# Gate steps at two places of a slot, stores and copies in other slots, residual loads by GpSimd, first and last parts reordered, in a one-core decoder layer

## The chip, the cores and the metric

The kernel runs on one core of a Trainium2 chip. A core has five engines that work side by side and signal one another with semaphores: TensorE (PE in the profile; its weight loads are PEld), VectorE (DVE), ScalarE (ACT), GpSimd (POOL) and SyncE (SP). SP issues DMAs only; ACT and POOL issue some too (a line with ACTq or SPq is such an issue). Each engine takes its instructions in the order in which they stand in its queue. The metric is the device time of one execution in microseconds.

## The reference

One layer of a decoder, in f32, for 512 prompt tokens and 8 sampled tokens, 520 columns in all, with a model width of 2048 and an FFN width of 5632:

```python
def conv_ffn(xn, prev, w_up, conv_w, conv_b, w_down):
    u, v = jnp.split(xn @ w_up, 2, axis=-1)
    cu, new = causal_dwconv(u, prev, conv_w)
    h = jax.nn.silu(cu + conv_b) * v
    return h @ w_down, new

m, c_new, s_new = mixer(rmsnorm(x, norm_mix_g[l]), conv_prev[l], gla_prev[l], w_in[l], ...)
x = x + m
f, f_new = conv_ffn(rmsnorm(x, norm_ffn_g[l]), ffn_prev[l], w_up[l], ...)
x = x + f
return rmsnorm(x, final_norm_g), ...
```

`mixer` projects with `w_in`, runs a gated convolution and a gated linear attention (GLA) with a state, and projects with `w_out`. `causal_dwconv` has width 3; the last two rows of its input are outputs as well.

## The kernel before

**Products.** Every f32 operand is split in two parts, `hi` (rounded, by ACT) and `lo` (the rest, by DVE), and a product is three matmuls: hi·hi, lo·hi, hi·lo. A matmul has a stationary 128x128 block of weights and 260 moving columns, half of the 520.

**Stages.** To 68 us: x is transposed tile by tile (`x_tile`), while the first products over `w_in` (one column block of q and one of k) run over the 16 tiles, with the norm's factors and the gate's low-rank product behind. To 600 us: the rest of `w_in`, GLA and convolution. To 870: `w_out`, and sums of x for the FFN. From 871 to 1812 the FFN's up phase, to 2227 its down phase, and to 2302 the last part: the last four FFN tiles, the residual and the final norm, in two halves of the columns (`half`).

**The up phase** has 44 tiles `t`. Each is a Strassen-Winograd product: seven products of half size instead of eight, in the order 1, 5, 6, 2, 7, 3, 4 (`ORDER`). Product `i` fills a slot of 24 matmuls on PE; `r` is its number in the scheme and `j` its place, `i % 7`. The weights of some products are sums of blocks, made on DVE, one of them in place in a single buffer `s` (5 to 6 to 3). The loop writes each slot in this order:

```python
        if i:
            (up_finish if i <= NU else down_finish)(i - 1)
        (up_product if kind == "up" else down_product)(i)
        prepare(i + 2)
```

then the gate's steps that are due, then `tick()`, which flushes collected state rows. `prepare(i + 2)` splits the weights of the product two slots later: hi by ACT (L1048), the next sum (L1012) and lo (L1052) by DVE. `up_finish(i - 1)` combines the last product's bank; after r = 3 it multiplies by the norm factor R (L1132) and calls `keep_last`, whose ACT copy (L522) takes the last rows of z.

`gate(t)` is a generator with the steps of a tile after its products; its yields are numbers of slots since the slot j = 0 of the next tile. Convolution taps (ACT L459, DVE L464 and L467), Silu (L1161), v·R (L1163), h = Silu·v (L1167); on odd t four half operations that make Strassen sums of h from two tiles (L1179 to L1181, with L1057), then four calls of `stored`: hi by ACT into one of two `fh` buffers, lo by DVE, two DMAs by POOL (L1146) to `f_d`.

**The down phase** has 5 chunks c of 4 groups g of 7 products, with the operands read back from `f_d` (`load_form`, L1213) into eight slots. `load_residual` (L1227) reads the residual into accumulators, `drain` writes the remaining flat rows of the convolution state (L537), and `load_last` brings the last tiles' h back (L1239, POOL).

**Order.** The FFN loop calls `InOrder`, which holds the program's order on PE, DVE and ACT. POOL and SP are ordered by a scheduler, as is everything outside the loop. Buffers: three each for hi, lo and raw weights, eight in `tmp`, two in `fh`, one for the last part's `y`.

Of the kernel before, what the change touches and what calls it, by code (L numbers as in the profile page):

```python
# [17 lines left out]
P = 128  # L18
D = 2048
# [18 lines left out]
def trunk_kernel(  # L38
# [18 lines left out]
    class InOrder:  # L57
# [5 lines left out]
        def __init__(self):  # L63
            self.count, self.last = len(self.all()), {}
# [128 lines left out]
    xa = []  # L193
    for k in range(KD):
        if k < KD // 2:
            xa.append([(quarter(bigA, f"x{s}{k}"), quarter(b12p, f"x{s}{k}b")) for s in "hl"])
        else:
            xa.append(
                [halves(bigA.tile([P, T], F32R, tag=f"x{s}{k}", name=f"x{s}{k}")) for s in "hl"]
            )  # L200
# [38 lines left out]
    def make_masks(mkp):  # L239
        nc.vector.tensor_copy(idn8, idn)  # L240
        for s in LEVELS:
# [15 lines left out]
            nc.vector.tensor_copy(masks[s], mf)  # L257


    with ExitStack() as es:  # L260
# [41 lines left out]
        cols = (3584, 3072)  # L302
        nc.scalar.dma_start(prow[0:16, :], norm_mix_g[0].rearrange("(k p) -> k p", p=P))
        load_x(xc[0][0], 0)
        nc.scalar.dma_start(xs, x_sample)
        load_x(xc[0][1], P)
        ws = [[load(w_in, 0, 4, c0, P) for c0 in cols]]
        for j in (2, 3):
            load_x(xc[0][j], j * P)
        r0 = 16  # L310
# [9 lines left out]
        for _ in range(8):  # L320
            nc.tensor.matmul(first[0][0][:, :P], ones, ones, start=True, stop=True)

        part = sp.tile([P, 4, 7], F32, name="part")
# [8 lines left out]
        def x_tile(k):  # L332
# [55 lines left out]
        for k in range(2):  # L388
            x_tile(k)
        ws = [[parts(*r) for r in ws[0]]]  # L390
        for k in range(KD):
            c, t = k // 4, k % 4
            if t == 0 and c < 3:
                load_x(xc[c + 1], (c + 1) * 512)
                ws.append([piece(w_in, 4 * c + 4, 4, c0, P) for c0 in cols])
            for ps, w in zip(first, ws[c]):
                span(ps, w, xa, k, 4 * c, 1, KD)
            if k + 2 < KD:
                x_tile(k + 2)
            junk = tmp()  # L400
# [9 lines left out]
            if c == 1:  # L410
# [8 lines left out]
            if k == 14:  # L419
                param_columns()  # L420
        nc.vector.reduce_sum(var[:, 0:4], part, axis=mybir.AxisListType.X)
        nc.vector.reduce_sum(var[:NS, 4:5], parts_s, axis=mybir.AxisListType.X)
        rs, tn, vv = (sp.tile([P, 5], F32, name=f"rs{i}") for i in range(3))
        rsqrt(var, D, vv, rs, tn, nc.vector)
        state_columns()
# [17 lines left out]
        make_masks(sp)  # L443

# [71 lines left out]
    def keep_last(z, j, n, new_p, new_s, get=None):  # L516
# [8 lines left out]
        if jj == n - 1:  # L525
            lt, c0 = last[0], (j - n + 1) * P

            def out():
# [6 lines left out]
                for r in range(10):  # L535
                    dst = new_p[0, 0, r] if r < 2 else new_s[0, r - 2, 1]
                    nc.sync.dma_start(  # L537
# [554 lines left out]
    def up_finish(i):  # L1092
# [37 lines left out]
        elif r == 3:  # L1130
            add(z2, bk["f"], st["c"])
            nc.vector.tensor_tensor(z2, z2, R[:, HT:], op=ALU.mult)  # L1132
            keep_last(st["z"], t, 11, new_ffn_p, new_ffn_s, mm_bank)
# [3 lines left out]
    def stored(src, dst):  # L1137

        n = src.shape[1]
        hi = wxp.tile([P, T], F32R, tag="fh", name="fh")[:, :n]  # L1140
        split(src, hi, src.bitcast(F32R))
        for d, x in zip(dst, (hi.bitcast(F32), src)):
# [5 lines left out]
    def gate(t):  # L1148

        st = state.pop((t,))  # L1150
        z, v = st["z"], st["v"]
        if not t:

            nc.vector.tensor_tensor(z[:, 2 : 2 + T], z[:, 2 : 2 + T], R, op=ALU.mult)
            keep_last(z, t, 11, new_ffn_p, new_ffn_s, mm_bank)
# [7 lines left out]
        nc.vector.tensor_tensor(v[:, :T], v[:, :T], R, op=ALU.mult)  # L1163
        yield 3
# [3 lines left out]
        yield 4  # L1168
        if t >= NF - CH:
            stored(h, hl_d[t - NF + CH])  # L1170
            return
# [4 lines left out]
        i = t // 2 % 4  # L1176
        t21, t34 = tmp()[:, :T], tmp()[:, :T]
# [308 lines left out]
```

## Time and profile before

| what | us |
|---|---|
| median of three runs | 2307.78 (2306.12 to 2309.48) |
| the profiled execution's own time | 2303.64 |
| its span, from first to last instruction | 2301.9 |
| up phase, from the first to the last product with R | 912.2 to 1810.5 |

The profile was taken of a single execution, and all durations are its own. A row of a timeline has the start, the duration in us (of one piece, with its count behind), engine, line and operation, and in brackets how long the engine had been idle before it and what released it. A row of waits has the total, the number and the longest. A row of windows has the stretch, its length, then the busy us with counts of PE, PEld, DVE, ACT and POOL, the clock granted to PE, the busy share of the DMA engines and GB/s. The chain is the work that ended last, traced back.

### The profile page before, as it was taken

The numbers are of one execution on the slowest core, as the hardware profiler recorded it, in microseconds if no ns is written. First come the engines' busy times: TensorE is split into PE (matmuls) and PEld (weight loads), VectorE is DVE, ScalarE is ACT, GpSimd is POOL, SyncE is SP. The second block draws the span as 40 slices with busy tenths as digits, with TensorE's granted clock in tenths as the row PEclk, the third lists the DMA queues.
The fourth block names the chain that finished last, engine by engine and source line by source line (L and its number), as shares of the span: only waits on it lengthen the run. The fifth ranks groups of instructions, "written<-read, shape, count | busy, mean of one in ns | idle before, by whom it ended". The sixth has DMA issues, their size and how long they took to land.

```text
span 2301.9 us, 43686 instructions
## 1 busy us (share of the span) xinstructions
PE 2225.7 (97%) x18131; PEld 2189.2 (95%) x18131; DVE 1625.2 (71%) x2168; ACT 998.2 (43%) x1429; POOL 305.1 (13%) x398
## 2 busy tenths in 40 slices
PE   8999999999999999999999999999999899999996
PEld 7999999999999999999999999999998899999996
DVE  6446455543434448888888898888888778888886
ACT  5334433312223335455455455455445444444445
POOL 2113223100001212011111011111111200000110
PEclk9999999999999999999999999999999999999998
DMA  7443344333455563555555555465464876764734
GB/s 215 116 129 109 103 118 120 95 92 92 112 152 157 166 192 100 143 138 140 148 149 138 137 156 140 129 165 140 124 164 134 286 239 198 231 199 144 220 111 139
DMA packets 455683, 344.06 MB, mean 149 GB/s; under 512 B 17673, under 2 KB 429733, under 8 KB 455341
## 3 DMA queue, kind: packets, MB, share of 16 engines
q1 hardware_dynamic: 438625, 288.25, 44.4%
q0 software_dynamic: 15536, 50.80, 7.1%
q8 instruction: 142, 2.33, 0.4%
q10 hardware_dynamic: 1324, 2.23, 0.3%
q14 instruction: 56, 0.46, 0.1%
HBM read 278.15 MB, written 63.27 MB: 148 GB/s over the span
## 4 chain that ended last, share of the span: by engine, by line
PE 55%; DVE 30%; issue 6%; ACT 5%; DMA 2%; POOL 1%; SPq 0%; ACTq 0%; DVEq 0%; POOLq 0%
PE mm L133 32%; DVE lo L1052 13%; PE y L1259 6%; PE x L1259 6%; DVE s L1012 6%; ACT hi L1048 4%; PE f L1259 2%; PE e L1259 2%; DVE raw L1012 2%; PE mm L1080 2%; DVE t L464 1%; DVE t L1167 1%; PE ms L720 1%; DVE t L117 1%; DVE zpad L1132 1%
## 5 line engine op out<-in xcount | busy, mean ns | idle before, releaser
L1080 PE MATMUL mm<-yh,hi 128*128 128x260 f32 x1408 | 402.4, 286 | 4.3 <-DVE t L1060 4.3
L1080 PE MATMUL mm<-yl,hi 128*128 128x260 f32 x1408 | 399.3, 284 | 0.0
L1080 PE MATMUL mm<-yh,lo 128*128 128x260 f32 x1408 | 398.4, 283 | 0.0
L1052 DVE TENSOR_TENSOR lo<-s,hi 128x1024 fp32r<-128x1024 f32 x192 | 238.6, 1243 | 147.4 <-ACT hi L1048 147.4
L1048 ACT ACTIVATE hi<-raw 128x1024 fp32r<-128x1024 f32 x256 | 270.0, 1055 | 165.4 <-PE mm L1080 61.0
L1052 DVE TENSOR_TENSOR lo<-raw,hi 128x1024 fp32r<-128x1024 f32 x256 | 316.4, 1236 | 11.8 <-ACT hi L1048 11.8
L104 ACT ACTIVATE hi<-raw 128x1024 fp32r<-128x1024 f32 (+1 forms) x148 | 152.7, 1033 | 392.3 <-PE mm L133 381.9
L105 DVE TENSOR_TENSOR lo<-raw,hi 128x1024 fp32r<-128x1024 f32 (+1 forms) x148 | 185.9, 1257 | 190.7 <-ACT hi L104 180.0
L133 PE MATMUL mm<-xh,hi 128*128 128x260 f32 (+2 forms) x1280 | 313.5, 294 | 4.9 <-ACT xh L119 2.6
L1048 ACT ACTIVATE hi<-s 128x1024 fp32r<-128x1024 f32 x192 | 202.7, 1056 | 245.3 <-DVE s L1012 205.5
L133 PE MATMUL mm<-xh,lo 128*128 128x260 f32 (+2 forms) x1280 | 303.7, 285 | 0.0
L133 PE MATMUL mm<-xl,hi 128*128 128x260 f32 (+2 forms) x1280 | 302.0, 283 | 0.9 <-DVE xl L120 0.5
L1080 PEld LDWEIGHTS mm<-yh,hi 128*128 128x128 f32 x1408 | 265.3, 188 | 10.2 <-ACT hi L1048 4.5
L1080 PEld LDWEIGHTS mm<-yh,lo 128*128 128x128 f32 x1408 | 266.0, 189 | 0.0
L1080 PEld LDWEIGHTS mm<-yl,hi 128*128 128x128 f32 x1408 | 265.7, 189 | 0.0
L133 PEld LDWEIGHTS mm<-xh,hi 128*128 128x128 f32 x1280 | 216.7, 190 | 15.4 <-issue 8.8
L1080 PE MATMUL ms<-xh,lo 128*128 128x260 f32 x704 | 203.9, 290 | 25.8 <-DVE lo L1052 25.7
L133 PEld LDWEIGHTS mm<-xl,hi 128*128 128x128 f32 x1280 | 217.4, 190 | 1.6 <-DVE xl L120 1.5
L133 PEld LDWEIGHTS mm<-xh,lo 128*128 128x128 f32 x1280 | 216.0, 189 | 0.3 <-DVE lo L105 0.2
L1080 PE MATMUL ms<-xh,hi 128*128 128x260 f32 x704 | 199.5, 283 | 1.7 <-ACT xh L116 1.7
L1080 PE MATMUL ms<-xl,hi 128*128 128x260 f32 x704 | 199.6, 283 | 0.5 <-DVE xl L117 0.5
L1080 PEld LDWEIGHTS ms<-xh,lo 128*128 128x128 f32 x704 | 133.3, 189 | 34.0 <-DVE lo L1052 34.0
(386 smaller groups left out, 5139.5 us busy)
## 6 DMA issues: line engine op xcount, KB each, us to landing
raw<-in_w_up_dram SPq DMA_DIRECT2D x176, 512.0 KB
raw<-in_w_down_dram SPq DMA_DIRECT2D x96, 512.0 KB
raw<-in_w_in_dram SPq DMA_DIRECT2D x92, 512.0 KB
form<-f_d SPq DMA_DIRECT2D x140, 260.0 KB
f_d<-fh POOLq DMA_DIRECT2D x60, 260.0 KB, 6.9
f_d<-t POOLq DMA_DIRECT2D x60, 260.0 KB, 6.3
raw<-in_w_out_dram SPq DMA_DIRECT2D x28, 512.0 KB
xT_d<-t SPq DMA_DIRECT2D x16, 260.0 KB
```

Of the source, the lines that this page charges most:

```text
L104: nc.scalar.activation(hi, raw, AF.Copy)
L105: nc.vector.tensor_tensor(lo, raw, hi.bitcast(F32), op=ALU.subtract)
L117: nc.vector.tensor_tensor(lo, src, hi.bitcast(F32), op=ALU.subtract)
L133: nc.tensor.matmul(o, w, xx, start=first and i == 0, stop=last and i == 2)
L464: nc.vector.scalar_tensor_tensor(c[:, :NP], z[:, i : i + NP], tap(i), c[:, :NP], op0=ALU.mult, op1=ALU.add)
L720: nc.tensor.matmul(pb[:, c * 64 : (c + 1) * 64], L[:, c, :], rhs[:, c], start=True, stop=True,)
L1012: return lambda: nc.vector.tensor_tensor(out, x, y, op=ALU.add)
L1048: nc.scalar.activation(his[i], src, AF.Copy)
L1052: nc.vector.tensor_tensor(los[i], src, his[i].bitcast(F32), op=ALU.subtract)
L1080: nc.tensor.matmul(st["bank"][b], w[:, k, :], x, start=b not in st["used"] and k == 0 and j == 0, stop=k == 7 and j == 2, skip_group_check ...
L1132: nc.vector.tensor_tensor(z2, z2, R[:, HT:], op=ALU.mult)
L1259: nc.tensor.matmul(ps[:, m, :], w[:, k, m * P : (m + 1) * P], x, start=b not in st["used"] and k == 0 and j == 0, stop=k == 3 and j == 2, ...
```

## The change

The gate's steps now run at two places in a slot, ahead of `prepare` (whole numbers) and behind it (halves): v·R comes first, the taps follow behind `prepare` in the same slot, Silu and the copy of the last rows come one slot later, h two slots after that, the half operations at 7, ahead of `prepare`, and the stores at 8.5, 10.5, 11.5 and 14. The third store takes its hi from `tmp` instead of `fh`. In chunk 0 the lo halves of the forms, the residual and the flat rows are loaded and stored by GpSimd, the flush before the down phase comes two slots later, and the residual is loaded behind the forms. In the first part, the weights of both columns are loaded into one tile right behind x's first block, x is copied from PSUM to SBUF before it is split, the masks' casts are GpSimd's, `InOrder` covers this part too, GpSimd included, and the table of ln and exp is loaded early. In the last part that table is loaded once ahead of it, and each half has its own `y`.

```diff
-        def __init__(self):
+        def __init__(self, *more):
+            self.engines += more
...
-        nc.vector.tensor_copy(idn8, idn)
+        nc.gpsimd.tensor_copy(idn8, idn)
...
+        def load_w(c):
+            raw = wp.tile([P, 1024], F32, tag="raw", name="raw")
+            for c0, r in zip(cols, (raw[:, :512], raw[:, 512:])):
+                nc.sync.dma_start(
...
-        load_x(xc[0][1], P)
-        ws = [[load(w_in, 0, 4, c0, P) for c0 in cols]]
-        for j in (2, 3):
+        nc.scalar.preload_act_table_set("natural_log_exp_and_others")
+        raws = [load_w(0)]
+        for j in (1, 2, 3):
             load_x(xc[0][j], j * P)
...
-            for b in range(2):
-                split(ps[:, b * HT : (b + 1) * HT], xa[k][0][b], xa[k][1][b], gm[:, k : k + 1])
-            st = tmp()
-            nc.vector.tensor_copy(st[:, :T], ps[:, :T])
-            nc.sync.dma_start(xT_d[k], st[:, :T])
+            st = tmp()[:, :T]
+            if k < 4:
+                nc.scalar.activation(st, ps[:, :T], AF.Copy)
+            else:
+                nc.vector.tensor_copy(st, ps[:, :T])
+            if k < KD // 2:
+                for b, src in enumerate(halves(st)):
+                    split(src, xa[k][0][b], xa[k][1][b], gm[:, k : k + 1])
+            else:
+                split(st, xw[0, k], xw[1, k], gm[:, k : k + 1])
+            nc.sync.dma_start(xT_d[k], st)
...
-        for k in range(2):
-            x_tile(k)
-        ws = [[parts(*r) for r in ws[0]]]
+        x_tile(0)
+        warm(8)
+        ws = [parts(raws[0], 8)]
+        x_tile(1)
+        in_order()
...
-                    nc.sync.dma_start(
+                    (nc.gpsimd if get else nc.sync).dma_start(
...
-            keep_last(st["z"], t, 11, new_ffn_p, new_ffn_s, mm_bank)
         elif r == 4:
...
-    def stored(src, dst):
+    def stored(src, dst, hi=None):
...
         z, v = st["z"], st["v"]
+        if t:
+            nc.vector.tensor_tensor(v[:, :T], v[:, :T], R, op=ALU.mult)
+        yield 0.5
...
         conv_rest(c, z, fcw, NF, t, stf[:, t, :])
-        yield 1
+        yield 1.5
         s = tmp()
         nc.scalar.activation(s[:, :T], c[:, :T], AF.Silu)
-        yield 2
-        nc.vector.tensor_tensor(v[:, :T], v[:, :T], R, op=ALU.mult)
-        yield 3
+        keep_last(
+            z, t, 11, new_ffn_p, new_ffn_s,
+            lambda: seeded["f"][:, :512] if t == NF - 1 else mm_bank(),
+        )
+        yield 3.5
...
+        yield 7
         t21, t34 = tmp()[:, :T], tmp()[:, :T]
...
-        yield 8
+        yield 8.5
         stored(b11, [dst[6, x, i] for x in range(2)])
-        yield 10
+        yield 10.5
         stored(t21, [dst[0:2, x, i] for x in range(2)])
-        yield 11
-        stored(t34, [dst[2:4, x, i] for x in range(2)])
-        yield 15
+        yield 11.5
+        stored(t34, [dst[2:4, x, i] for x in range(2)], tmp())
+        yield 14
         stored(h, [dst[4:6, x, i] for x in range(2)])
...
-                nc.sync.dma_start(
+                (nc.sync, nc.gpsimd)[x if c == 0 else 0].dma_start(
...
-            nc.sync.dma_start(
+            nc.gpsimd.dma_start(
                 two(acc[g, q]),
...
+    def run_steps(now):
+        for s in list(steps):
+            while s and s[1] + s[2] <= now:
...
-        prepare(i + 2)
         if 1 <= n <= NF and j == 0:
             steps.append([gate(n - 1), i, 0])
...
+        run_steps(i)
...
+        prepare(i + 2)
+        run_steps(i + 0.5)
         tick()
...
-            if j == 6:
-                drain()
         if kind == "down":
             c, g = at
+            if c == 0 and g == 0 and j == 1:
+                drain()
             if c == 0 and j == 0:
                 if g == 0:
-                    load_residual(0)
                     for x in (4, 5, 6):
                         load_form(0, x)
+                    load_residual(0)
...
+    tables = nc.scalar.preload_act_table_set("natural_log_exp_and_others")
...
-        fin = fp.tile([P, len(tiles), D], F32, name="y")
+        fin = fp.tile([P, len(tiles), D], F32, name=f"y{b}")
```

**VectorE at the turn of a tile.** The rows run from the product of z with R (slot j = 6, last row of the tile before) to the taps of that tile. `s`, `raw`, `hi`, `lo` belong to the weights of coming products, `t` to the gate; a row has line, operation, output and inputs, shape. Before:

```order
L1132 TENSOR_TENSOR zpad_880<-zpad_880,R 128x260
L1052 TENSOR_TENSOR lo<-s,hi 128x1024
L1012 TENSOR_TENSOR s<-s,raw 128x1024
L1052 TENSOR_TENSOR lo<-s,hi 128x1024
L464 SCALAR_TENSOR_TENSOR t<-zpad_880,parf,t 128x512
```

And of the change, where the half operations stand in every second tile:

```order
L1165 TENSOR_TENSOR zpad_855<-zpad_855,R 128x260
L1085 TENSOR_TENSOR lo<-s,hi 128x1024
L1045 TENSOR_TENSOR s<-s,raw 128x1024
L1220 TENSOR_TENSOR t<-t 128x260
L1090 SCALAR_TENSOR_TENSOR t<-t 128x260
L1222 TENSOR_TENSOR t<-t 128x260
L1090 SCALAR_TENSOR_TENSOR t<-t 128x260
L1188 TENSOR_TENSOR t<-t,R 128x520
L1085 TENSOR_TENSOR lo<-s,hi 128x1024
L497 SCALAR_TENSOR_TENSOR t<-zpad_855,parf,t 128x512
```

Between the sum in place and the second `lo` now stand v·R and, in such tiles, the four half operations.

**ScalarE at the same place.** `last` is the copy of the last rows. Before:

```order
L522 ACTIVATE last<-zpad_881 128x10
L1048 ACTIVATE hi<-s 128x1024
L1135 ACTIVATE t<-mm 128x260
L1048 ACTIVATE hi<-s 128x1024
L459 ACTIVATE t<-zpad_881,parf 128x520
```

And of the change:

```order
L1081 ACTIVATE hi<-s 128x1024
L1167 ACTIVATE t<-mm 128x260
L1081 ACTIVATE hi<-s 128x1024
L492 ACTIVATE t<-zpad_855,parf 128x520
L1123 ACTIVATE ms<-mm 128x260
L1081 ACTIVATE hi<-raw 128x1024
L117 ACTIVATE fh<-t 128x260
L1199 ACTIVATE t<-t 128x520
L555 ACTIVATE last<-zpad_855 128x10
```

The copy has moved from ahead of the first hi to behind Silu.

**SyncE and GpSimd between up and down.** SP before, from the first forms on (`flat` are the state's rows, `acc` the residual):

```order
L1213 DMA form<-f_d_9530 128x2x260 x13
L1008 DMA raw<-in_w_down_dram 128x4x256
L537 DMA out_dram<-flat 11x128 x10
L1008 DMA raw<-in_w_down_dram 128x4x256 x3
L1227 DMA acc<-x_d 128x2x260 x4
L1213 DMA form<-f_d_9530 128x2x260 x12
L1227 DMA acc<-x_d 128x2x260 x4
```

POOL of the change:

```order
L1254 DMA form<-f_d_9504 128x2x260 x8
L1180 DMA hh_d_9513<-fh 128x520
L1180 DMA hl_d_9514<-t 128x520
L1268 DMA acc<-x_d 128x2x260 x4
L1254 DMA form<-f_d_9504 128x2x260 x6
L1268 DMA acc<-x_d 128x2x260 x5
L570 DMA out_dram<-flat 11x128 x10
```

The flat rows stand on POOL now, behind its share of the forms and nine of the residual's loads; SP keeps the weights and the other half of the forms.

More of the change, by code (lines that the diff above doesn't have):

```diff
@@ L197, in trunk_kernel @@
         else:
[L198 to L200 removed]
+            for i, s in enumerate("hl"):
+                xw[i, k] = bigA.tile([P, T], F32R, tag=f"x{s}{k}", name=f"x{s}{k}")
+            xa.append([halves(xw[i, k]) for i in range(2)])
     xT_d = dp.tile([KD, P, T], F32, name="xT_d")
@@ L319, in trunk_kernel, with warm @@
         first = [new_mm() for _ in cols]
-        for _ in range(8):
-            nc.tensor.matmul(first[0][0][:, :P], ones, ones, start=True, stop=True)
+        def warm(n):
+            for _ in range(n):
+                nc.tensor.matmul(first[1][1][:, :P], ones, ones, start=True, stop=True)
+        warm(8)
+        in_order = InOrder(nc.gpsimd.engine)
         part = sp.tile([P, 4, 7], F32, name="part")
@@ L1317, in trunk_kernel @@
         (up_product if kind == "up" else down_product)(i)
[L1318 to L1324 removed]
         if 1 <= n <= NF and j == 0:
             steps.append([gate(n - 1), i, 0])
[L1327 to L1332 removed]
+        run_steps(i)
+        if i in (NU, NU + 2):
+            x, ps = xd[0, 1][0][0], seeded["e" if i == NU else "f"]
+            for m in range(2):
+                nc.tensor.matmul(inner(ps)[:, m, :], x[:, :P], x, start=True, stop=True)
+        prepare(i + 2)
+        run_steps(i + 0.5)
         tick()
```

69 lines of the change are left out of this document (42 added, 27 removed).

## The prediction

> **What bounds the kernel now.** I read the page's busy line first, then what TensorE (PE) waited for, then each stage at the scale of one step.
>
> ```profile
> PE 2225.7 (97%) x18131; PEld 2189.2 (95%) x18131; DVE 1625.2 (71%) x2168; ACT 998.2 (43%) x1429; POOL 305.1 (13%) x398
> ```
> ```profile
> PE ms L1080 <- DVE lo L1052: 25.7, 39, 0.7
> PE x L1259 <- DMA form<-f_d: 8.4, 2, 6.7
> ```
>
> PE looks full, and these waits, its two longest, are 34 us together (in all, times, longest). But ends of pipelined matmuls are modelled, so PE can look busy while it loses. I therefore measure FFN tiles from a DVE (VectorE) instruction that runs once per tile, the product with R at L1132.
>
> ```profile
> L1132 DVE TENSOR_TENSOR zpad<-zpad,R x43: 429/430/433, 912.2 to 1810.5; 128x260 f32<-128x260 f32 x43
> ```
> ```profile
> 1743.67 0.43 DVE L1132 TENSOR_TENSOR zpad<-zpad,R 128x260 f32<-128x260 f32 x1
> 1769.62 0.43 DVE L1132 TENSOR_TENSOR zpad<-zpad,R 128x260 f32<-128x260 f32 x1
> 1790.34 0.43 DVE L1132 TENSOR_TENSOR zpad<-zpad,R 128x260 f32<-128x260 f32 x1
> 1810.45 0.43 DVE L1132 TENSOR_TENSOR zpad<-zpad,R 128x260 f32<-128x260 f32 x1
> ```
>
> From 912.2 to 1810.5 lie 42 tiles in 898.3 us. One took 25.95 (1743.67 to 1769.62), the last two 20.72 and 20.11, the other 39 so (898.3 - 66.8) / 39 = 21.32 each. Yet 20.11 was possible, 168 matmuls at 0.120 us. What holds the others is the engine that makes operands:
>
> ```profile
> 1000.00:1100.00 100.00, 96.64 (x789) 95.00 (x788) 88.79 (x118) 52.12 (x76) 12.23 (x18) 1.00 0.54 142
> ```
> ```profile
> 1018.53 0.43 DVE L1132 TENSOR_TENSOR zpad<-zpad,R 128x260 f32<-128x260 f32 x1
> 1020.18 1.22 DVE L1052 TENSOR_TENSOR lo<-s,hi 128x1024 fp32r<-128x1024 f32 x1 [1.23 <-ACT hi L1048]
> 1021.44 1.23 DVE L1012 TENSOR_TENSOR s<-s,raw 128x1024 f32<-128x1024 f32 x1
> 1023.85 1.23 DVE L1052 TENSOR_TENSOR lo<-s,hi 128x1024 fp32r<-128x1024 f32 x1 [1.19 <-ACT hi L1048]
> ```
> ```profile
> 1018.99 0.22 ACT L522 ACTIVATE last<-zpad 128x10 f32<-128x10 f32 x1 [4.77 <-DVE zpad L1132]
> 1019.11 1.04 ACT L1048 ACTIVATE hi<-s 128x1024 fp32r<-128x1024 f32 x1
> 1022.76 1.06 ACT L1048 ACTIVATE hi<-s 128x1024 fp32r<-128x1024 f32 x1 [2.33 <-DVE s L1012]
> ```
>
> The third number of the first row is DVE: 88.79 of 100 us, so 18.9 of a 21.32 us tile. The rest is two gaps per tile, 1.23 and 1.19. In the first, ACT (ScalarE) has been idle for 4.77 us, because the small copy at L522 stands ahead of the hi copy in ACT's queue and needs DVE's product of 1018.53. Hi comes late, so lo, the sum made in place, the next hi and the next lo come late in a chain. The second gap is that chain itself: sum, hi, lo with nothing else for DVE. Two products later PE misses its third operand (the 25.7 us row). So DVE's loop with its two gaps bounds this phase, not PE.
>
> **Up phase.** The change moves L522's copy behind Silu, one slot later, so ACT makes hi as soon as its sum is there: the first gap's cause goes. It puts v*R, and alternately the half ops or a split, between the sum and the second lo. A 520-wide operation:
>
> ```profile
> 1031.48 0.69 DVE L1163 TENSOR_TENSOR t<-t,R 128x520 f32<-128x520 f32 x1
> 1032.09 1.22 DVE L1052 TENSOR_TENSOR lo<-s,hi 128x1024 fp32r<-128x1024 f32 x1
> 1056.63 0.42 DVE L1179 TENSOR_TENSOR t<-t 128x260 f32<-128x260 f32 x1
> ```
>
> It costs 0.61 from start to start (1031.48 to 1032.09), the four half ops some 4 x 0.37 = 1.5 (an estimate from that row's 0.42 less an overlap). The second gap of 1.19 is then filled by 0.61 + 1.5 or by 2 x 0.61, with work that DVE did elsewhere in the tile. DVE needs 18.9 us then, or 20.1 if one gap of 1.2 stayed; PE needs 20.11 and takes over as the bound. If all 42 tiles ran at 20.11, 898.3 would become 844.6: 53.7 at most. A conv tap still waits on ACT and a split still stands in a queue now and then, so I take 50; ends 0 and 53.7. Part of it is the one stopped tile:
>
> ```profile
> 1765.27 0.64 ACT L116 ACTIVATE fh<-t 128x520 fp32r<-128x520 f32 x1 [6.60 <-DMA f_d<-fh]
> ```
> ```profile
> f_d<-fh POOLq DMA_DIRECT2D x60, 260.0 KB, 6.9
> ```
>
> There ACT waited 6.60 us for a store to free one of two fh buffers: 25.95 - 20.11 = 5.84 us of delay, and part of the 53.7. A slot is 24 matmuls, 20.11 / 7 = 2.87 us. Before, a pair's splits stand at steps 8, 10, 11 and 15, each with its own fh, so the third needs the first one's buffer 3 slots, 8.6 us, later, and a store takes 6.9 us to land after its issue: a margin of 1.7 us for the issue and its queue. Now the third split has its hi in another pool, and the three others stand at 8.5, 10.5 and 14: the nearest reuse is 5.5 slots or 15.8 us. What becomes tight is that other pool, with eight buffers; counting its users per pair, its nearest reuse leaves about one slot, 2.9 us. Ten flat-row stores, four times in the phase, go from SP's queue to GpSimd's and can eat that; a cover gone costs up to 5.84, four times. My 3.7 below the most allows for that in part. A loss in this phase needs the stop in many tiles (rival d), since DVE and ACT get no instruction that they did not have.
>
> **Up to down.** SP's queue and what PE did:
>
> ```profile
> 1812.83 7.77 SPq L537 DMA_DIRECT2D out_dram<-flat  x10
> 1824.91 10.25 SPq L1213 DMA_DIRECT2D form<-f_d  x12
> ```
> ```profile
> 1818.00:1820.00 2.00, 2.00 (x19) 2.00 (x18) 2.00 (x4) 1.15 (x3) 0.00 (x0) 1.00 0.04 12
> 1834.00:1836.00 2.00, 1.69 (x8) 1.69 (x9) 0.00 (x0) 0.00 (x0) 1.00 (x2) 0.50 1.11 376
> ```
> ```profile
> 1813.14 0.51 PE L1259 MATMUL x<-form,hi 128*128 128x260 f32 x2 [0.64 <-ACT t L1135]
> 1839.20 2.86 PE f L1259 x24
> ```
>
> Ten small stores hold SP for 7.77 us, in which the DMA engines are all but empty (share 0.04, 12 GB/s in the first window). The forms behind them leave from 1824.91 on; PE waits 8.4 us, and when it resumes its granted clock is 0.50 (second window). Five products from 1813.14 should end at 1813.14 + 5 x 2.87 = 1827.5; the sixth starts at 1839.20: 11.7 lost.
>
> After the change the stores are GpSimd's, and stand behind the loads that the first group needs. The forms leave when product 4 frees their slots, near 1812, half of each by SP and half by GpSimd. About 10 MB (28 half-forms of 0.26 MB, five weights of 0.5, four residuals; an estimate) are to be moved from 1798 on; at the 376 GB/s of the second window that is 28 us, to 1826, against a last need of the fifth and sixth products' forms between 1824 and 1830 with PE at full clock. The margin is about 3 us and I take 10.5, ends 0 and 11.7. What is late next is the residuals: they are needed by the first sums behind the group, and a product lies between. GpSimd's own issues cost this:
>
> ```profile
> 1005.02 0.71 POOL L1146 DMA_DIRECT2D f_d<-fh  x1 [10.06 <-ACT fh L116]
> ```
>
> DVE was busy while it issued. The Trainium skill ("SBUF — State Buffer", section "SBUF: two separate sides", its box on the "DVE blocks DMA" trap) says the opposite can happen: descriptors of DMAs from GpSimd's queue wait while VectorE runs certain two-port copies. By that rule the forms would come late; the rival below prices it from rows. No such wait shows in this trace.
>
> **Start.** PE's first steps:
>
> ```profile
> 8.87 1.29 DVE L105 TENSOR_TENSOR lo<-raw,hi 128x512 fp32r<-128x512 f32 x2 [7.75 <-ACT hi L104]
> 10.22 0.16 DVE L330 COPY gm<-tp 128x16 f32<-128x16 f32 x1
> 10.44 1.11 PE L335 MATMUL tp<-idn,x 128*128 128x128 f32 x4 [4.34 <-DVE gm L330]
> 14.19 0.58 PE L133 MATMUL mm<-xh,hi 128*128 128x260 f32 x1 [1.48 <-ACT xh L119]
> 18.00:19.00 1.00, 1.00 (x6) 0.65 (x4) 0.00 (x0) 0.00 (x0) 0.00 (x0) 0.50 1.12 314
> 68.59 0.36 PE L133 MATMUL mm<-xh,hi 128*128 128x260 f32 x1 [1.27 <-DVE k L452]
> ```
>
> A tiny copy (10.22) stands behind two weight splits on DVE, which themselves wait for ACT and the weights, and costs PE 4.34. Another wait costs 1.48. From 10.44 to 19 PE runs at a clock of 0.50: 19 - 10.44 - 1.48 = 7.1 us of matmuls that need half of that, 3.5 too much. With the 1.27 ahead of the first v product (68.59), behind the norm factor's chain of reciprocal roots, these are 10.6 us.
>
> Now the tiny copy is first on DVE, the casts of masks are GpSimd's, and both columns' first weights are one load and one split. The path to the first product becomes: transposes, copy to SBUF by ACT (about 0.7 by the 0.69 of a 520-wide operation), two splits for x, hi and lo of the weights (1.04 and 1.23 as in the up phase). If ACT starts near 6.9, where its own small loads end, the first product comes at 6.9 + 0.7 + 1.0 + 1.0 = 9.6 rather than 14.19 (its first column ran from 11.68), with a warm clock. Against that stand eight more warm-up matmuls (sixteen passes in the trace, 3.78 us at the start's clock, so 1.9 at twice that), and possibly two waits of 1 us for weights that arrive behind x:
>
> ```profile
> 1.13 3.78 PE L321 MATMUL mm<-ones 128*128 128x128 f32 x16 [1.13 <-DVE zpad L508]
> ```
>
> I take 7. Ends: 10.6, and -2 if those two waits are all that comes of it.
>
> **Last part.**
>
> ```profile
> 2260.00:2270.00 10.00, 8.97 (x75) 8.54 (x74) 7.66 (x19) 8.99 (x15) 0.00 (x0) 1.00 0.69 231
> 2270.00:2280.00 10.00, 7.89 (x68) 7.72 (x68) 5.79 (x11) 4.94 (x11) 0.00 (x0) 1.00 0.40 129
> ```
> ```profile
> 2276.14 2.48 DVE L1400 TENSOR_TENSOR y<-ms,gf 128x512 f32<-128x512 f32 x4 [2.69 <-DMA out_dram<-y]
> 2289.70 1.28 ACT L230 ACT_TABLE_LOAD   x1
> 2291.22 1.28 ACT L231 ACT_TABLE_LOAD   x1
> ```
>
> Two table loads lie behind the last matmul: 2 x 1.28 = 2.6, all exposed, and go. A second y buffer ends DVE's wait of 2.69 for a store; PE lost 1.03 + 2.11 = 3.1 in the two windows, of which I take 2.4. The rest of those windows is ACT's own row of work, 8.99 of 10 us. Together 5, ends 2.6 and 2.6 + 3.1 = 5.7. In this trace 0.24 us lie between the first load's end (2290.98) and the second's start. The Trainium skill ("ScalarE: Activation LUTs", "What ACT_TABLE_LOAD costs") adds a drain of about 1.38 us to each; by it the end would save about 5.3 instead of 2.6. No drain shows here.
>
> Mixer, w_out and the later down chunks keep their orders: 0. **Sum: 50 + 10.5 + 7 + 5 = 72.5 us.** The profiled execution took 2303.64 (span 2301.9 and 1.74 around it), so it would become 2231; the runs' median, 2307.78, is 4.1 above it. Same saving from the median: 2307.78 - 72.5 = 2235.
>
> **Rivals.**
> (a) DVE's loop keeps a new late chain, say the half ops delay lo and then hi at the same place. For: the margin is about 20.1 - 18.9 = 1.2 us per tile and the half ops alone are 1.5. Against: they come in every second tile, where the chain's wait of 1.19 covers most of them. Half the gain stays lost: 2235 + 25 = 2260.
> (b) GpSimd's issues at the boundary are held up behind DVE's operations: four residuals and six half-forms, each by one operation of 1.23, is 12.3 us, 9.3 beyond the margin of 3: 2235 + 9.3 = 2244. For: DVE has 2.00 of 2 us busy in the window at 1818. Against: the 0.71 us above.
> (c) The start gives nothing, because its order is now written out per step and two weight splits stand ahead: 2242, inside the forecast's spread.
> (d) Slower. The stop of 1758 to 1765 (ACT waits at the head of its queue for a buffer) returns in each pair of tiles, because stores lie closer together: 20 x 5.84 = 117, less the gains, 2235 + 117 = 2352. It decides from 72.5 / 5.84 = 12.4 of 20 pairs. Against: it happened once in 20 before.
> (e) The edit moves nothing on DVE because data, not order, ties it: 2307.78 - 10.5 - 7 - 5 = 2285. Against: L522's wait of 4.77 is an order wait; hi needs nothing of it.
>
> **How the numbers follow.** Forecast with (c) 0.76, (a) 0.10, (b) 0.07, (e) 0.04, (d) 0.03. All ends at their best save 53.7 + 11.7 + 10.6 + 5.7 = 81.7: 2226, and a run varies by about 2 (2306.12 to 2309.48), so low is 2223 with 1 for what I rounded; high is 2263, to hold (a), (b) and (c). Outside stay (d), (e) and odd sums, below 0.2. A measurement tells about 0.2% (4.6 us) from no change. Faster by more 0.96, within 0.01, slower 0.03.
>
> **What would show it.** Right: tiles of 20.1 to 20.2 between successive products with R; no row of PE waiting for lo; no gaps of 1.2 before lo; in the boundary no wait over 1 us and a clock of 1.00; the first split matmul near 10 and the row at 68.59 six to eight earlier; no table load behind the last matmul, no wait for y's store. Wrong: tiles near 20.7 with a DVE gap left (a); waits for forms (b); ACT waiting for stores of fh (d).

## The result and the profile after

| | before | after |
|---|---|---|
| median of the runs, us | 2306.95 (4 runs, 2305.23 to 2309.48) | 2249.36 (4 runs, 2246.44 to 2251.89) |
| profiled execution, us | 2303.64 | 2246.44 |
| its span, us | 2301.9 | 2244.7 |

The ratio is 0.9749, with a 95% interval of 0.9732 to 0.9766: 57.6 us saved at the median, where 72.5 were forecast. The time lies in the stated range (2223 to 2263), 14 us above the predicted one. Each stage has a mark in both traces (the first v product, the first and last product with R, the first matmul of the last part, the end), so the two profiled executions can be subtracted stage by stage:

| stage | before | after | saved | forecast |
|---|---|---|---|---|
| to the first v product | 68.59 | 67.86 | 0.7 | 7 |
| from there to the first product with R | 843.6 | 843.5 | 0.1 | 0 |
| 42 FFN tiles, first to last product with R | 898.2 | 846.7 | 51.5 | 50 |
| from there to the last part (boundary and down) | 417.1 | 417.5 | -0.4 | 10.5 |
| last part | 74.4 | 69.2 | 5.2 | 5 |

Two terms came as forecast, two came hardly or not at all. The page of the changed kernel, its busy line and the engine line of its chain, then the group view of the product with R (now L1165; min, median and max ns, then its first and last start):

```profile
PE 2203.6 (98%) x18147; PEld 2181.6 (97%) x18147; DVE 1627.4 (72%) x2144; ACT 1004.4 (45%) x1417; POOL 350.6 (16%) x476
...
PE 92%; DVE 3%; DMA 2%; ACT 1%; issue 1%; POOL 1%; ACTq 0%; SPq 0%; DVEq 0%; POOLq 0%
```
```profile
L1165 DVE TENSOR_TENSOR zpad<-zpad,R x43: 429/430/433, 911.3 to 1758.1; 128x260 f32<-128x260 f32 x43
```

The busy shares hardly moved; the chain did, from 55% on PE and 30% on DVE to 92% on PE. The engine line before:

```profile
PE 55%; DVE 30%; issue 6%; ACT 5%; DMA 2%; POOL 1%; SPq 0%; ACTq 0%; DVEq 0%; POOLq 0%
```

The tiles take 846.7 / 42 = 20.16 us, 0.05 above the period that was forecast for a PE that waits for nothing. The same 100 us as before in windows, and DVE at the turn of a tile:

```profile
1000.00:1100.00 100.00, 100.00 (x836) 100.00 (x835) 93.67 (x124) 54.05 (x79) 10.93 (x17) 1.00 0.51 144
```
```profile
1012.08 0.43 DVE L1165 TENSOR_TENSOR zpad<-zpad,R 128x260 f32<-128x260 f32 x1
1012.63 1.22 DVE L1085 TENSOR_TENSOR lo<-s,hi 128x1024 fp32r<-128x1024 f32 x1
1013.89 1.22 DVE L1045 TENSOR_TENSOR s<-s,raw 128x1024 f32<-128x1024 f32 x1
1015.03 0.42 DVE L1220 TENSOR_TENSOR t<-t 128x260 f32<-128x260 f32 x1
...
1016.52 0.70 DVE L1188 TENSOR_TENSOR t<-t,R 128x520 f32<-128x520 f32 x1
1017.13 1.22 DVE L1085 TENSOR_TENSOR lo<-s,hi 128x1024 fp32r<-128x1024 f32 x1
```

Neither lo has a bracket any more: both gaps are gone, PE is busy 100 of 100 us with 836 matmuls where there were 789, and DVE does the same work in less time (93.67 of 100).

At the boundary nothing improved. What PE waited for, SP's queue, and two windows, one inside the wait and one behind it:

```profile
PE x L1300 <- DMA form<-f_d: 8.3, 1, 8.3
```
```profile
1746.70 5.26 SPq L1254 DMA_DIRECT2D form<-f_d  x8
1752.07 14.08 SPq L1041 DMA_DIRECT2D raw<-in_w_down_dram  x3
1766.25 16.38 SPq L1254 DMA_DIRECT2D form<-f_d  x10
```
```profile
1774.00:1776.00 2.00, 0.00 (x0) 0.00 (x0) 2.00 (x4) 0.89 (x2) 1.09 (x3) 1.00 1.03 350
1780.00:1784.00 4.00, 2.44 (x11) 2.47 (x12) 0.00 (x0) 0.00 (x0) 3.90 (x6) 0.50 1.10 358
```

The flat rows have left SP, yet SP's half of the forms of products 4 to 6 still leaves only at 1766.25. On the clock of before, 52.4 us later by the last product with R, that is 1818.6. GpSimd's half leaves from 1761.29 on, which is 1813.7 on that clock. Ahead of SP's half stand three weight loads of the next group, 14.08 us in issue, because they wait for buffers that VectorE still reads. SP's longest wait from 1752 to 1766, and GpSimd's first such form:

```profile
SPq L1041 <- DVE lo L1085: 5.8, 1, 5.8
```
```profile
1761.29 0.71 POOL L1254 DMA_DIRECT2D form<-f_d  x1 [0.44 <-issue]
```

And the DMA engines are now full throughout (1.03 in the first window), where they were nearly empty from 1818 to 1822 before (a share of 0.00 to 0.12 in each microsecond). When PE goes on, its granted clock is 0.50 again (second window), and the first product takes 5.54 us instead of 2.87. The wait of 8.3 and these 2.7 make 11.0, about what was lost at this place before (11.7).

### The profile page after: what moved, and what is told of

Same layout as the page of the kernel before. It is cut to its first block, busy times and chain, and to the rows that moved or that the text cites. A ratio compares the mean times of both kernels' runs of the same rounds, so it can differ in the third digit from the quotient of the medians.

```text
span 2244.7 us, 43607 instructions
## 1 busy us (share of the span) xinstructions
PE 2203.6 (98%) x18147; PEld 2181.6 (97%) x18147; DVE 1627.4 (72%) x2144; ACT 1004.4 (45%) x1417; POOL 350.6 (16%) x476
## 3 DMA queue, kind: packets, MB, share of 16 engines
q10 hardware_dynamic: 1324, 2.23, 0.3%
## 4 chain that ended last, share of the span: by engine, by line
PE 92%; DVE 3%; DMA 2%; ACT 1%; issue 1%; POOL 1%; ACTq 0%; SPq 0%; DVEq 0%; POOLq 0%
PE mm L134 32%; PE mm L1113 28%; PE ms L1113 11%; PE x L1300 6%; PE y L1300 6%; PE f L1300 3%; PE e L1300 2%; PE ms L753 1%; DMA form<-f_d 1%; PE ms L739 0%; PE tp L284 0%; DVE lo L106 0%; DMA xT_d<-t 0%; PE ms L821 0%; PE ms L835 0%
## 5 line engine op out<-in xcount | busy, mean ns | idle before, releaser
L1081 ACT ACTIVATE hi<-raw 128x1024 fp32r<-128x1024 f32 x256 | 271.1, 1059 | 203.5 <-PE mm L1113 56.3
L1085 DVE TENSOR_TENSOR lo<-raw,hi 128x1024 fp32r<-128x1024 f32 x256 | 317.2, 1239 | 21.3 <-ACT hi L1081 21.2
L105 ACT ACTIVATE hi<-raw 128x1024 fp32r<-128x1024 f32 x144 | 152.0, 1056 | 392.2 <-PE mm L134 380.0
L106 DVE TENSOR_TENSOR lo<-raw,hi 128x1024 fp32r<-128x1024 f32 x144 | 184.8, 1283 | 182.2 <-ACT hi L105 171.8
L1045 DVE TENSOR_TENSOR s<-s,raw 128x1024 f32<-128x1024 f32 x128 | 156.7, 1224 | 2.2
```

Of the source, the lines that this page charges most:

```text
L105: nc.scalar.activation(hi, raw, AF.Copy)
L106: nc.vector.tensor_tensor(lo, raw, hi.bitcast(F32), op=ALU.subtract)
L1045: return lambda: nc.vector.tensor_tensor(out, x, y, op=ALU.add)
L1081: nc.scalar.activation(his[i], src, AF.Copy)
L1085: nc.vector.tensor_tensor(los[i], src, his[i].bitcast(F32), op=ALU.subtract)
```

## The experiments

The first two ask which of the two gaps mattered in the up phase. **Copy back**: only the copy of the last rows returns to its old place (tile 0 apart).

```diff
         elif r == 3:
             nc.vector.tensor_tensor(z2, z2, R[:, HT:], op=ALU.mult)
+            keep_last(st["z"], t, 11, new_ffn_p, new_ffn_s, ...)
...
         nc.scalar.activation(s[:, :T], c[:, :T], AF.Silu)
-        keep_last(z, t, 11, new_ffn_p, new_ffn_s, ...)
+        if not t:
+            keep_last(z, t, 11, new_ffn_p, new_ffn_s, mm_bank)
```

> The changed kernel with one edit undone: the ACT copy of the last rows stands again directly behind the product with R, ahead of the next hi copy, and the gate's other steps stay where the change put them. In the changed kernel 42 tiles took 846.7 us between products with R (20.16 each). Theory A (VectorE's loop had two gaps and closing either one of them lets TensorE bound the phase): one gap of about 1.2 us comes back, VectorE needs 18.9 + 1.2 = 20.1 us per tile, the phase takes 847 to 863 us. Theory B (the copy alone was the cause, the steps between the sum and lo do nothing): the old time, 890 to 900 us. Theory C (filling the second gap was what counted): 846 to 849 us with no new gap on VectorE.

Measured: 863.7 us for the 42 tiles. DVE of this kernel at two tile turns:

```profile
1042.11 0.43 DVE L1165 TENSOR_TENSOR zpad<-zpad,R 128x260 f32<-128x260 f32 x1
1043.77 1.23 DVE L1085 TENSOR_TENSOR lo<-s,hi 128x1024 fp32r<-128x1024 f32 x1 [1.23 <-ACT hi L1081]
...
1061.78 0.43 DVE L1165 TENSOR_TENSOR zpad<-zpad,R 128x260 f32<-128x260 f32 x1
1063.44 1.23 DVE L1085 TENSOR_TENSOR lo<-s,hi 128x1024 fp32r<-128x1024 f32 x1 [1.23 <-ACT hi L1081]
```

The first gap is back to the hundredth, but costs 17 us instead of 51. Tiles alternate between 21.35 and 19.67, mean 20.5: the slow ones hold the half operations between sum and lo. Theory B falls; A is nearest, 0.7 us above its range.

**Copy alone**: the kernel of before, with the copy moved behind Silu and nothing else.

```diff
             nc.vector.tensor_tensor(z2, z2, R[:, HT:], op=ALU.mult)
-            keep_last(st["z"], t, 11, new_ffn_p, new_ffn_s, mm_bank)
+            if t == NF - 1:
+                keep_last(st["z"], t, 11, new_ffn_p, new_ffn_s, mm_bank)
...
         nc.scalar.activation(s[:, :T], c[:, :T], AF.Silu)
+        if t < NF - 1:
+            keep_last(z, t, 11, new_ffn_p, new_ffn_s, mm_bank)
```

> The kernel of before with one edit: the ACT copy of the last rows moves behind Silu for tiles 0 to 42; all other gate steps, stores, start, boundary and last part are those of before. Before, 42 tiles took 898.3 us. Theory A (either gap closed is enough): 850 to 866 us, with one tile still stopped by a buffer of fh (about 6 us). Theory B (the copy is the whole cause): the same 850 to 860. Theory C (only the filled second gap counts): 885 to 898 us, and the row of TensorE waiting for lo stays near 25 us.

Measured: 849.2 us, 0.8 below what A and B said, and a run of 2259.81 beside 2305.25. Its group view of the product with R and the DVE row behind it:

```profile
L1132 DVE TENSOR_TENSOR zpad<-zpad,R x43: 429/430/431, 916.0 to 1765.2; 128x260 f32<-128x260 f32 x43
```
```profile
1021.26 1.22 DVE L1052 TENSOR_TENSOR lo<-s,hi 128x1024 fp32r<-128x1024 f32 x1 [1.19 <-ACT hi L1048]
```

The second gap stands as it was, 1.19, and 49 of 51.5 us are gone all the same, by a copy of ten columns. Theory C falls. What is left of the 51.5 is not the second gap: the first 39 tiles take 786.6 us here and 786.3 in the changed kernel, 20.17 and 20.16 each. The other 2.2 us lie in the last three tiles, one of which takes 24.09, because ACT waits there for a buffer of `fh`:

```profile
1722.34 0.64 ACT L116 ACTIVATE fh<-t 128x520 fp32r<-128x520 f32 x1 [4.79 <-DMA f_d<-fh]
```

So closing the first gap frees the loop wholly; the other gate steps of the change, with the copy put back, free it by about two thirds.

**Forms by GpSimd** separates the two causes that the boundary has left, SP's queue and the bytes.

```diff
-                (nc.sync, nc.gpsimd)[x if c == 0 else 0].dma_start(
+                (nc.gpsimd if c == 0 and (x or j > 3) else nc.sync).dma_start(
```

> The changed kernel with one edit: for chunk 0 both halves of the forms of products 4 to 6 are loaded by GpSimd, so none of them stands on SP's queue behind the three weight loads of the next group, which wait there until 1766 us for buffers. In the changed kernel TensorE waits 8.3 us for a form and 417.5 us lie between the last product with R and the first matmul of the last part. Theory queue (the forms were late because of SP's weight loads): wait 0 to 3 us, 417.5 becomes 406 to 410. Theory bytes (the DMA engines are full from 1750 to 1790, so the forms land no earlier whoever issues them): wait 6 to 9 us, 415 to 418.

Measured: 410.5 us, 7.0 less, and no wait for a form. PE's waits from 1755 to 1810, and SP there:

```profile
PE y L1300 <- DVE lo L1085: 2.3, 1, 2.3
PE x L1300 <- DVE acc L1314: 0.8, 1, 0.8
```
```profile
1757.02 15.49 SPq L1041 DMA_DIRECT2D raw<-in_w_down_dram  x3
1772.68 9.58 SPq L1254 DMA_DIRECT2D form<-f_d  x4
```

SP is held as long as before (15.49 us), with nothing urgent behind it. The queue was the main cause. What is left is a wait of 2.3 us for the lo of weights that come late: the load on the chain left SP at 1766.63 and landed 20.09 us later, with the DMA engines full (1.06 from 1757 to 1787). So bytes are part of the rest, and SP's wait for buffers, which stands ahead of that load, may be another. The result lies half a microsecond outside what the queue theory said.

**Residual behind**: the same kernel, with the residual on SP, behind those weight loads.

```diff
-            nc.gpsimd.dma_start(
+            nc.sync.dma_start(
                 two(acc[g, q]),
```

> The kernel of the third experiment (both halves of the forms of products 4 to 6 by GpSimd) with one more edit: the residual is loaded by SP again, where it stands behind the three weight loads that wait for buffers, so 4 loads of 0.26 MB go behind the forms. In the third experiment 410.5 us lie between the last product with R and the last part, no form is waited for, and TensorE waits 2.3 us for a lo whose weights came late and 0.8 us for the residual's sum. Theory bytes at the end (DMA engines full, what is loaded first is what counts): less in front, weights earlier, the 2.3 us go, 407 to 409. Rival (weights come when their buffers come free, the order of the rest is nothing): 410 to 412. If the residual now comes late itself: a wait for the sum with it of more than 2 us, 412 or more.

Measured: 413.3 us, the third case. DVE waits for the residual, and TensorE with it; but TensorE also waits for a form again:

```profile
DVE acc L1314 <- DMA acc<-x_d: 6.7, 2, 6.2
```
```profile
1782.27 0.39 PE L1300 MATMUL f<-form,hi 128*128 128x260 f32 x1 [1.28 <-DMA form<-f_d]
1787.96 0.55 PE L1300 MATMUL x<-form,hi 128*128 128x260 f32 x2 [2.68 <-issue]
```

The second row starts right behind the sum that the late residual held up (1787.16, 0.69 long). The first has another reason: GpSimd's order changed with the edit. Four loads of the last tiles' h now stand ahead of the forms there, wait 5.92 us for a store to land, and the forms leave at 1768.67 and 1773.85. So the experiment does not price the residual alone; it shows that it can't go last for free.

**v weights later**: ACT's hi copies of the first v group must follow its work on x.

```diff
+        after_start.append(in_order.last[nc.scalar.engine])
...
         ws = [piece(w, k0, 8, c0, P) for k0 in (0, 8)]
+        if after_start:
+            name = after_start.pop()
+            for i in nc.cur_bb.bb.instructions[-6:]:
+                if i.engine == nc.scalar.engine:
+                    tc.add_manual_dep(i, name, ..., reason="in order")
```

> The changed kernel with one edit: the hi copies of the first v group's weights, which ACT takes at 44.9 and 47.7 us in the middle of x's last tiles, must follow ACT's last work of that loop. In the changed kernel the first v matmul starts at 67.86 us (68.59 before). Theory ACT queue (these two copies, 2 x 1.04, and their lo, 2 x 1.23, delay x tiles 12 to 14 and with them all behind): first v matmul at 65.3 to 66.5. Rival (the products are paced by the serial chain copy, hi, lo of each tile, or the norm's factors come last): 67.3 to 69.

Measured: 67.47, by the letter the rival's case. But the yardstick of 67.86 was a lucky one. Six other kernels here share the changed start word for word, and their first v product comes later, from 69.44 to 73.56. ACT in the execution of the copy-back kernel:

```profile
44.06 1.04 ACT L105 ACTIVATE hi<-raw 128x1024 fp32r<-128x1024 f32 x1
...
48.64 1.06 ACT L105 ACTIVATE hi<-raw 128x1024 fp32r<-128x1024 f32 x1 [2.31 <-DMA raw<-in_w_in_dram]
51.45 1.04 ACT L105 ACTIVATE hi<-raw 128x1024 fp32r<-128x1024 f32 x1
```

And its first v product in PE's timeline:

```profile
73.56 0.39 PE L134 MATMUL mm<-xh,hi 128*128 128x260 f32 x1 [1.18 <-DVE k L485]
```

The v weights have not landed, and ACT stands at the head of its queue with x's last tiles behind. Over the seven executions with this start:

| ACT's wait for the v weights, us | first v product, us |
|---|---|
| none (the changed kernel's profile) | 67.86 |
| 1.34 | 69.44 |
| 1.24 | 70.25 |
| 1.31 | 70.26 |
| 1.07 | 70.38 |
| 2.05 | 71.46 |
| 2.31 | 73.56 |

The longest waits go with the latest products, but the order is not strict (1.34 stands above 1.07), so the wait is not all of the spread. The median is 70.26, against 68.59 and 68.86 in the two profiles of the old start. So the new start is some 1.5 us slower as a rule, and with the v weights later it is 2.8 better than that median. One execution each for the variants; the spread says how far that goes.

**Split from PSUM**, on top of that: the copy to SBUF goes behind the split again.

```diff
-            if k < 4:
-                nc.scalar.activation(st, ps[:, :T], AF.Copy)
-            else:
-                nc.vector.tensor_copy(st, ps[:, :T])
             if k < KD // 2:
-                for b, src in enumerate(halves(st)):
+                for b, src in enumerate(halves(ps)):
                     split(src, xa[k][0][b], xa[k][1][b], gm[:, k : k + 1])
             else:
-                split(st, xw[0, k], xw[1, k], gm[:, k : k + 1])
+                split(ps[:, :T], xw[0, k], xw[1, k], gm[:, k : k + 1])
+            if k < 4:
+                nc.scalar.activation(st, ps[:, :T], AF.Copy)
+            else:
+                nc.vector.tensor_copy(st, ps[:, :T])
```

> The kernel of the fourth experiment (v weights' hi copies behind ACT's work on x) with one more edit: x's tiles are split straight from PSUM, as before the change, and copied to SBUF behind that. In the fourth experiment tile 15 is transposed at 51.6 us, tiles follow each other at 2.23 us where nothing is in the way, and the first v matmul starts at 67.5. Theory chain (transpose, copy 0.69, hi 0.73, lo 0.76, product in one row set the pace of a tile): tiles at 1.9 to 2.1 us and the first v matmul at 63.5 to 66. Rival (TensorE's own 2.05 us per tile or the loads of x set it): 66.5 to 68.5.

Measured: 64.76. The time is that of the chain theory, not its reason: tiles still follow at 2.23 us, and PE is busy in all of 15.57 us from tile 8 to tile 15, so that is TensorE's own pace. What went are the longer steps between tiles: 3.8 us from tile 9 to 10 and 3.3 from 12 to 13 in the changed kernel and in the kernel with the v weights later alike.

**No preload**: the last part without its one table load.

```diff
-    tables = nc.scalar.preload_act_table_set("natural_log_exp_and_others")
-    tc.add_manual_dep(tables.ins, last_act.name, ..., reason="in order")
```

> The changed kernel without the one load of the ln and exp table ahead of the last part; the two buffers for y stay. In the changed kernel the last part takes 69.2 us from its first matmul to the end of the span (74.4 before), and no table is loaded in it. Theory: four table loads of 1.28 us return, two of them behind the last matmul, so 71.5 to 72; the two in the middle cost TensorE nothing, since y of the second half has its own buffer. Rival (the loads in the middle were what held TensorE before): 73 to 74.5. By the page's drain of 1.38 us per load the end would cost about 5.3 us instead of 2.6.

Measured: 73.56 us for the last part, so the rival's case: the two loads in the middle cost as well. ACT behind the last matmul of this kernel:

```profile
2242.01 0.30 ACT L230 ACTIVATE fin<-fin,eps_t 128x3 f32<-128x3 f32 x1 [0.85 <-DVE fin L1476]
2242.33 1.28 ACT L231 ACT_TABLE_LOAD   x1
...
2243.84 1.28 ACT L232 ACT_TABLE_LOAD   x1
...
2246.17 0.72 ACT L1482 ACTIVATE y<-y,fin 128x512 f32<-128x512 f32 x1 [0.82 <-DVE fin L226]
```

And the same place in the changed kernel:

```profile
2234.42 0.30 ACT L230 ACTIVATE fin<-fin,eps_t 128x3 f32<-128x3 f32 x1 [0.85 <-DVE fin L1484]
...
2236.01 0.72 ACT L1490 ACTIVATE y<-y,fin 128x512 f32<-128x512 f32 x1 [0.83 <-DVE fin L226]
```

From 2242.01 to 2246.17 are 4.16 us, where the changed kernel has 1.59. The end costs 2.57, two loads of 1.28.

**One y**: one buffer for both halves again.

```diff
-        fin = fp.tile([P, len(tiles), D], F32, name=f"y{b}")
+        fin = fp.tile([P, len(tiles), D], F32, name="y")
```

> The changed kernel with one edit undone: one buffer for y in both halves of the last part; the table of ln and exp is still loaded once ahead of it. The last part took 74.4 us before, 69.2 in the changed kernel (69.4 to 70.2 in five others with the same last part) and 73.6 without the one load of the table. Theory (the table loads held ACT and with it TensorE in the middle, too; the second buffer adds little): 69.8 to 71. Rival (the wait for y's store, 2.7 us on VectorE before, is a cost of its own): 71.5 to 73.

Measured: 71.66 us, again the rival's case. DVE's wait is back, and costs about 2 us:

```profile
2228.85 2.48 DVE L1454 TENSOR_TENSOR y<-ms,gf 128x512 f32<-128x512 f32 x4 [3.55 <-DMA out_dram<-y]
```

Without the load the last part is longer by some 4 us, without the buffer by 2, and without both by 5, so part of the two seems to be the same time. The last part varies from 69.2 to 70.2 us among kernels that have both, so that overlap of about 1 us is not certain.

**Third split in fh**: the stop of one tile.

```diff
-        stored(t34, [dst[2:4, x, i] for x in range(2)], tmp())
+        stored(t34, [dst[2:4, x, i] for x in range(2)])
```

> The changed kernel with one edit undone: the third store's hi goes to one of the two fh buffers again; the stores stay at 8.5, 10.5, 11.5 and 14. In the changed kernel 42 tiles took 846.7 us and no tile of a pair's sum is over 41 us. Theory (the third split needs the first one's buffer 3 slots or 8.6 us later, a store lands 4 to 7 us after its issue, so the margin is small and a late store stops ACT and with it VectorE and TensorE): 1 to 6 stops of 3 to 6 us, 850 to 875. Rival (stores land in time, the stop before was one of a kind): 846 to 849.

Measured: 849.2 us, 2.4 more than the changed kernel, with a single stop in the pair at tile 41, as before the change:

```profile
1721.71 0.64 ACT L117 ACTIVATE fh<-t 128x520 fp32r<-128x520 f32 x1 [4.79 <-DMA f_d<-fh]
```

The rival is nearer: stores land in time in 19 of 20 pairs. Why only this one is late was not tried.

**Combined**: the two edits that helped at the boundary (forms by GpSimd) and at the start (v weights later, split from PSUM), together.

> The changed kernel with the edits of the third and the sixth experiment together: both halves of the forms of products 4 to 6 in chunk 0 by GpSimd, the v weights' hi copies behind ACT's work on x, x's tiles split from PSUM. They lie in different stages, so the savings should add: 417.5 to 410.5 us at the boundary (7.0) and the first v matmul at 64.8 us instead of 70.3 (median of six starts of the changed order; 5.5). From the changed kernel's median of 2249.4: 2249.4 - 12.5 = 2236.9, so 2234 to 2241, a ratio of 0.969 to 0.972 to the kernel of before. If the start's gain only moves a wait to the mixer behind it: 2240 to 2244.

Measured: 2240.91 us, median of 5 runs (2238.79 to 2244.21); ratio to before 0.9722, interval 0.9709 to 0.9736. It beats both kernels: all its runs lie below all of the changed one's (2246.44 to 2251.89), 8.5 us at the medians, though the two were not timed side by side. In its profile the first v product comes at 65.15 and boundary and down take 410.6, so both savings are there. Still 12.5 us were expected, and the result lies in both ranges. The mixer took 846.4, within the 843.5 to 847 that it varies by, so whether part of the start's gain became a wait there stays open.

## Why the prediction was right and where it was wrong

**Up phase: right in mechanism and size.** 51.5 us against 50, at most 53.7. That the copy at the head of ACT's queue starts the chain is shown by the copy moved alone (49 us). The other gate steps, the filled second gap above all, gave some 34 of 51 with the copy put back, some 2.4 of them by the stop that is gone. With the copy moved, they add nothing to a tile's time (20.17 us without them, 20.16 with them): the prediction counted on both gaps, and the first one was enough. The step "or 20.1 if one gap of 1.2 stayed; PE needs 20.11" holds for the second gap (20.17 us a tile); with the first gap left it is 863.7 / 42 = 20.56. Rival (a) did not come, nor (e).

**The one stop: mis-sized.** The third split's buffer gave 2.4 us, not 5.84, since a stop is partly caught up in the next tile (24.56 us, then 18.40, where the changed kernel has 20.87 and 19.42). With the copy's 49 us it makes up the whole 51.5. Rival (d), stops in many pairs, did not come in any kernel.

**Boundary: wrong, 10.5 forecast, -0.4 measured.** The step that failed: "The forms leave when product 4 frees their slots, near 1812". GpSimd's half did (1813.7 on that clock), but SP's half left at 1818.6, because the prediction looked at the ten stores on SP and not at what is next in that queue: three weight loads that wait for buffers. Its own estimate of bytes failed with it: 28 us for 10 MB from 1798 on, with a margin of 3. The items that it lists add up to 10.8 MB, and more was under way, nine residuals and last tiles' h among it: in the 35.8 us from there to the landing of the last form that PE waited for, the engines moved 12.0 MB, at 335 GB/s. That the queue counts is shown by moving the forms (7.0 us). That bytes count too is likely from the 20.09 us that a weight load then took; no experiment moved bytes alone. The time came out as rival (b) had it for this place, but not for its reason (GpSimd's timeline and the window around it, changed kernel):

```profile
1764.11 1.49 POOL L1254 DMA_DIRECT2D form<-f_d  x2 [0.33 <-PE x L1300]
```
```profile
1764.00:1766.00 2.00, 2.00 (x19) 2.00 (x18) 2.00 (x5) 1.60 (x3) 1.58 (x3) 1.00 1.04 350
```

Two issues in 1.49 us, while DVE was busy 2.00 of 2.00, and 0.70 for one of the same size at 1771.10, where DVE stood idle: GpSimd was not held up. The Trainium skill's rule on this ("SBUF — State Buffer", "SBUF: two separate sides", the box on the "DVE blocks DMA" trap) is about operations in a two-port mode, such as f32 copies from SBUF to SBUF; DVE's operations here each take two tensors (sums, lo splits and convolution taps), and nothing of it shows.

**Start: wrong, 7 forecast, 0.7 in this profile and about -1.5 as a rule.** The first steps did come sooner. PE of the changed kernel:

```profile
11.34 0.39 PE L134 MATMUL mm<-xh,hi 128*128 128x260 f32 x1 [2.76 <-ACT hi L105]
```

11.34 rather than 9.6, since ACT's small loads held it until 8.79, not 6.9: the early table load, 1.28 us at 1.96, now stands ahead of four of them. Nor was the clock warm; it was granted at 0.56 and 0.59 from 12 to 16. Up to tile 12 x's tiles were transposed 2.6 to 4.8 us earlier than before (tile 10 3.8), tile 15 0.2 later. So two steps failed: 7 us were never there, and what was there was carried to 68.59 as it stood. In between x's tiles pass through ACT, and waits of the kind that the prediction put at its low end of -2 ("for weights that arrive behind x", two of 1 us) are the rule, here for the v weights: in six of seven executions 1.1 to 2.3 us of waiting, and 2 us of hi copies, ahead of x's last tiles. In time this is rival (c), that the start gives nothing. The two start experiments both keep these copies behind x; split from PSUM takes 2.7 us more, so the copy ahead of the split was a cost too.

**Last part: right in size.** 5.2 against 5. The parts are as forecast at the end (2.57 against 2.6); the Trainium skill's drain behind a load ("ScalarE: Activation LUTs", "What ACT_TABLE_LOAD costs"), which would have made it about 5.3 by an estimate from that page, does not show. The two expectations written for it afterwards were wrong, in that each credited one edit with the middle; it belongs to both.

The sum missed by 72.5 - 57.2 = 15.3 in the profiled executions: 10.9 at the boundary and 6.3 at the start, less 1.8 that the other stages gave beyond their terms, with 0.1 of rounding. That the time still lies in the range is no merit of these two terms: the upper end of 2263 was set wide enough to hold rivals (a), (b) and (c).

## What to carry to other kernels

Where a small instruction stands in an engine's queue ahead of one that others wait for, read whether it waits: ten columns copied later, behind Silu, were worth 49 us. Before a queue is credited with a gain, read the next two things behind what is taken out of it, and what each waits for; and add up all bytes under way, not only those that the stage needs. And a gain at a stage's start counts only as far as the next queue that all later tiles pass.

## What was not expected of the hardware

One and the same start took from 67.86 to 73.56 us to the first v product in seven executions, latest where ACT waited longest for one load (2.05 and 2.31 us), though that wait is not all of it: a profile of one execution can flatter a change by several microseconds where a queue waits for a DMA. The mixer's 843.5 to 847 us vary as well, with the same instructions. And a table load costs 1.28 us, with 0.24 to the next, in which an operation of 0.20 runs: nothing else is visible around it.
